# Linear attention with ReLU features on one core: K and V of two groups loaded as one transfer of 256 rows

## Chip, cores and metric

The kernel runs on one core of one Trainium2 chip. The metric is the device time of one execution in microseconds, median of several. The time before is 126.63 us (three runs, 126.61 to 126.84). Engines are TensorE (PE, with its weight loads PEld), VectorE (DVE), ScalarE (ACT), GpSimd (POOL) and SyncE (SP); 16 DMA engines move data between the chip's memory (HBM) and the on-chip memory.

## What is computed

Q, K, V and the output have the shape 8 batches x 12 heads x 512 positions x 64, in fp32: 12.58 MB each. For each of the 96 heads a 64 x 64 matrix and a vector of 64 are summed over all positions of K and V, and each row of Q is multiplied with them.

```python
Q_feat = np.maximum(0, Q)
K_feat = np.maximum(0, K)
KV = np.einsum('bhkd,bhkv->bhdv', K_feat, V)
K_sum = np.sum(K_feat, axis=2)
numerator = np.einsum('bhqd,bhdv->bhqv', Q_feat, KV)
denominator = np.einsum('bhqd,bhd->bhq', Q_feat, K_sum)
return numerator / (denominator[:, :, :, None] + 1e-10)
```

## The kernel before

**Tiling.** Heads are taken in 24 groups of four, and two groups make an octet (12 of them). A group's K is one block of 512 KB in HBM, read as 128 rows of 4 KB: one row is 16 positions of one head, and 32 rows in a column are one head. In the on-chip memory a row is one partition. V is the same. An octet's Q is 1 MB in 128 rows of 8 KB. All loads but those of the first octet's K and V are issued by GpSimd and cast to bf16 on the way, so a K or V tile has 2 KB per partition and a Q tile 4 KB.

**Loads.** The four fp32 loads of groups 0 and 1 (`kv_first`, L106 and L107) are issued by SyncE. GpSimd issues Q of octet 0, then for octets 1 to 11 K, V of the even group, K, V of the odd group, and Q (`load_kv`, L92 to L96; `load_q`, L98; the loop at L110). These instructions stand in GpSimd's queue in this order from the start, each behind the waits for its buffer and for its place among the transfers in flight. The pools `kin` and `vin` have 12 buffers each, `qin` has 7.

**Work of an octet.** Order is written by hand, and each engine runs its instructions in that order.

- `prep(g)` (L133): DVE makes from K the two masked ReLU features (kf, two instructions at L136), and from V the half `vo` at L138. `prep_v` (L141) makes the other half, on ACT for the even group (L143) and on DVE for the odd one (L145).
- `mm_kv(g)` (L148): 16 matmuls sum K features times V into `ps_kv` (L150). `evac_kv` (L156) copies the result of both groups on ACT (L160).
- `qt(o)` (L181): PE transposes Q (L171), ACT applies ReLU (L179).
- `denom(o)` (L218): 16 small matmuls and three DVE instructions (L224, L229, L233) give the reciprocal denominators.
- `out_t(o)` (L193): eight matmuls (L201), copied by ACT (L203).
- `backs(o)` (L283): PE transposes the result back (L239) and DVE multiplies it with the reciprocals, two instructions at L245 (`norm`); then the store.

PSUM tiles of `out_t` and `back` share two buffers (`ps_out`). The loop at L297 runs for o from 0 to 9. For o from 1 to 8 it begins with `kvs(o)`, both `mm_kv` and the evacuation. Then come prep of group 2o+2, `backs(o - 1)`, `denom(o)`, `out_t(o)`, prep of group 2o+3 and `qt(o + 1)`. From o = 8 on `kvs(o + 1)` stands ahead of `qt(o + 1)`, and `backs(o)` behind it. The last two octets are written out from L314 on.

**Stores.** SyncE issues one store of 1 MB per octet (L260), the last octet's in two halves (L258). `store(o)` for o up to 6 is held back: ahead of it SyncE issues a tiny transfer, `scratch`, that reads K of group 2(o + 5) (L253) and so waits until that K tile has landed.

Of the kernel before, what the change touches and what calls it, by code (L numbers as in the profile page):

```python
# [10 lines left out]
def kernel(  # L11
# [7 lines left out]
    nc = tc.nc  # L19
    B, H, S, D = Q.shape  # L20
    assert D == 64
    P = 128
# [4 lines left out]
    R = S * 4 // P  # L27
# [4 lines left out]
    NO = NG // 2  # L32
    assert NO * 8 == NH and R == 16 and RQ == 32
    DELAY = 5
    F32 = 2

    fp32 = mybir.dt.float32
    bf16 = mybir.dt.bfloat16
# [3 lines left out]
    def pool(name, bufs, **kw):  # L42
        return ctx.enter_context(tc.tile_pool(name=name, bufs=bufs, **kw))

    consts = pool("consts", 1)
    qin = pool("qin", 7)
    kin = pool("kin", 12)
    vin = pool("vin", 12)
    kfp = pool("kfp", 4)
    rcp = pool("rcp", 2)  # L50
    outp = pool("outp", DELAY + 2)
# [6 lines left out]
    def view(X, f):  # L58
        return X.rearrange("b h s d -> (b h s d)").rearrange("(n p f) -> n p f", p=P, f=f)

    Qr, Kr, Vr, Or = view(Q, RQ * D), view(K, R * D), view(V, R * D), view(out, RQ * D)
# [27 lines left out]

    q_sb, k_sb, v_sb = {}, {}, {}  # L90

    def load_kv(g):  # L92
        k_sb[g] = kin.tile([P, R, D], bf16, name="k_sb")
        nc.gpsimd.dma_start(out=k_sb[g].rearrange("p r d -> p (r d)"), in_=Kr[g], single_packet=True)  # L94
        v_sb[g] = vin.tile([P, R, D], bf16, name="v_sb")
        nc.gpsimd.dma_start(out=v_sb[g].rearrange("p r d -> p (r d)"), in_=Vr[g], single_packet=True)  # L96

    def load_q(o):  # L98
        q_sb[o] = qin.tile([P, U, 2 * D], bf16, name="q_sb")
        nc.gpsimd.dma_start(out=q_sb[o].rearrange("p u f -> p (u f)"), in_=Qr[o], single_packet=True)  # L100


    for g in range(F32):
        kv = outp.tile([P, 2, R, D], fp32, name="kv_first", tag="o_sb")
# [3 lines left out]
    load_q(0)  # L108
    make_identity(nc, ident)
    for o in range(1, NO):  # L110
        load_kv(2 * o)
        load_kv(2 * o + 1)
        load_q(o)

    def zero(i):
# [198 lines left out]
    o = NO - 2  # L314
    g = 2 * NO - 2
# [52 lines left out]
```

## Time and profile before

| | |
|---|---|
| Median of the runs | 126.63 us (126.61 to 126.84) |
| The profiled execution, its own time | 126.52 us |
| its span, first to last instruction | 124.7 us |
| mean granted TensorE clock | 0.95 |
| PE, PEld busy | 86.0 us, 78.5 us (69%, 63% of the span) |
| DVE, ACT busy | 81.1 us, 79.3 us (65%, 64%) |
| POOL busy (issues of loads mostly) | 33.1 us (27%) |
| HBM read, written | 37.75 MB, 12.58 MB (403 GB/s over the span) |
| K loads by GpSimd | 22, 256 KB each (bf16), 13.9 us from issue to landing |
| V loads by GpSimd | 22, 256 KB each, 13.2 us |
| Q loads | 12, 512 KB each, 14.9 us |
| K issue, V issue on POOL | 578 ns, 597 ns |

A busy share is a mean over the whole span. The page also cuts the span into 40 slices of 3.1 us and gives for each the share of time in which the DMA engines were busy, in tenths (9 is 90% or more), the bytes that they moved per second, and the granted clock of TensorE. Loads that cast count with the bytes that they write, half of what they read. A queue's share is the time that its packets took, over 16 engines' span; packets of one engine overlap a little, so that the shares add up to a little over 100%. In a timeline each line is one or several instructions that follow one another: start, duration, engine, line of the kernel, what it writes and reads, and in brackets how long its engine sat idle before it and what ended that.

The granted clock over the 40 slices is full but for a few: `9999999999999999999769959958999999999996`.

### The profile page before, as it was taken

To read this page: it belongs to the slowest core of one execution; us is meant where nothing else is said; L and a number is where in the kernel's file an instruction comes from. 1 tells how busy PE (TensorE), PEld (TensorE's weight loads), DVE (VectorE), ACT (ScalarE), POOL (GpSimd) and SP (SyncE) were. 2 spreads that over 40 slices of the span, in tenths; PEclk is the share of its full clock that TensorE was granted. 3 is DMA by queue.
4 is the path that set the end of the run, shared out by engine and by line. 5 is a ranking of instruction groups with operands and counts; after the bars stand their busy time and mean duration, and the time that the engine had idled before them with its cause. 6 is when DMAs were issued, how large, how long until landed. Compare 5 with 4: busy or idle time off the path is not lost.

```text
span 124.7 us, 2672 instructions
## 1 busy us (share of the span) xinstructions
PE 86.0 (69%) x1075; PEld 78.5 (63%) x1075; DVE 81.1 (65%) x176; ACT 79.3 (64%) x114; POOL 33.1 (27%) x62
## 2 busy tenths in 40 slices
PE   0041196998989899894598599399777587797600
PEld 0040194997878788793597499299576486696500
DVE  2605743949798897979247845935928918979600
ACT  0251549989898997989249558666839646837100
POOL 6924433415253341142133124034022000000000
PEclk9999999999999999999769959958999999999996
DMA  3999999999999999999999999999999999999993
GB/s 133 322 285 277 216 205 210 213 210 215 207 213 208 210 214 327 257 215 300 282 215 282 302 213 258 324 213 234 342 223 218 322 257 215 319 416 420 426 416 143
DMA packets 10748, 32.68 MB, mean 262 GB/s; under 512 B 1392, under 2 KB 1392, under 8 KB 9328
## 3 DMA queue, kind: packets, MB, share of 16 engines
q0 software_dynamic: 8064, 17.83, 74.7%
q1 hardware_dynamic: 2672, 14.68, 29.2%
q8 instruction: 8, 0.13, 0.4%
q14 instruction: 4, 0.03, 0.1%
HBM read 37.75 MB, written 12.58 MB: 403 GB/s over the span
## 4 chain that ended last, share of the span: by engine, by line
DMA 34%; DVE 26%; PE 25%; ACT 5%; issue 2%; SPq 1%; DVEq 1%; ACTq 0%; POOLq 0%
DMA v_sb<-in_V_dram 14%; DVE o_sb L245 13%; DMA q_sb<-in_Q_dram 13%; PE ps_kv L150 11%; DMA kv_first<-in_V_dram 8%; PE ps_bk L239 6%; PE ps_qt L171 4%; DVE kf L136 3%; ACT qt L179 3%; DVE vo L138 3%; ACT kvd L160 2%; PE ps_ot L201 2%; DVE vo L145 2%; DVE den L229 1%; DVE rec L233 1%
## 5 line engine op out<-in xcount | busy, mean ns | idle before, releaser
L150 PE MATMUL ps_kv<-vo,kf 128*128 128x132 bf16 x384 | 31.3, 247 | 18.4 <-ACT vo L143 7.9
L150 PEld LDWEIGHTS <-kf 128*128 128x128 bf16 x384 | 28.9, 111 | 19.7 <-DVE vo L138 10.3
L245 DVE TENSOR_TENSOR o_sb<-ps_bk,rec 128x1024 f32<-128x1024 f32 x24 | 28.4, 1220 | 16.7 <-PE ps_bk L239 16.7
L160 ACT CAST kvd<-ps_kv 64x260 bf16<-64x260 f32 (+1 forms) x54 | 18.7, 346 | 19.0 <-PE ps_kv L150 16.8
L179 ACT ACTIVATE qt<-ps_qt 128x1024 bf16<-128x1024 bf16 x23 | 22.4, 1027 | 4.9 <-PE ps_qt L171 4.8
L203 ACT COPY ot_sb<-ps_ot 128x1024 f32<-128x1024 f32 x22 | 21.9, 1014 | 2.1 <-PE ps_ot L201 1.3
L239 PE MATMUL ps_bk<-ident,ot_sb 128*128 128x128 f32 x192 | 23.0, 273 | 0.0
L136 DVE TENSOR_SCALAR kf<-k_sb,mask 128x1024 bf16<-128x1024 bf16 x44 | 18.3, 457 | 5.8 <-DMA k_sb<-in_K_dram 5.8
L94 POOL DMA_DIRECT2D k_sb<-in_K_dram x22 | 12.7, 578 | 34.1 <-DMA q_sb<-in_Q_dram 16.8
L239 PEld LDWEIGHTS ps_bk<-ident,ot_sb 128*128 128x128 f32 x192 | 20.8, 141 | 0.0
L171 PE MATMUL ps_qt<-ident,q_sb 128*128 128x128 bf16 x192 | 15.3, 243 | 5.6 <-DMA q_sb<-in_Q_dram 5.6
L96 POOL DMA_DIRECT2D v_sb<-in_V_dram x22 | 13.1, 597 | 19.7 <-DMA k_sb<-in_K_dram 12.0
L171 PEld LDWEIGHTS <-q_sb 128*128 128x128 bf16 x192 | 13.7, 110 | 6.6 <-DMA q_sb<-in_Q_dram 6.4
L201 PE MATMUL ps_ot<-qt,kvd 128*128 128x256 bf16 x88 | 13.5, 284 | 4.0 <-DVE o_sb L245 4.0
L201 PEld LDWEIGHTS <-kvd 128*128 128x128 bf16 x88 | 8.5, 101 | 6.5 <-issue 5.4
L138 DVE TENSOR_SCALAR vo<-v_sb,mask 128x1024 bf16<-128x1024 bf16 x22 | 10.8, 489 | 1.6 <-DMA v_sb<-in_V_dram 1.6
L143 ACT ACTIVATE vo<-v_sb,mask 128x1024 bf16<-128x1024 bf16 x10 | 11.5, 1154 | 0.2
L221 PEld LDWEIGHTS <-qt 128*128 128x128 bf16 x192 | 6.7, 97 | 4.7 <-ACT qt L179 3.4
L221 PE MATMUL ps_den<-kvd,qt 128*128 128x16 bf16 x192 | 7.5, 179 | 2.6 <-ACT qt L179 2.1
L100 POOL DMA_DIRECT2D q_sb<-in_Q_dram x12 | 6.7, 558 | 8.0 <-DMA v_sb<-in_V_dram 5.0
L224 DVE SCALAR_TENSOR_TENSOR own<-ps_den,mask_h 128x256 f32<-128x256 f32 x12 | 5.0, 417 | 3.3 <-PE ps_den L221 3.3
L145 DVE TENSOR_SCALAR vo<-v_sb,mask 128x1024 bf16<-128x1024 bf16 x12 | 5.8, 484 | 0.0
(27 smaller groups left out, 29.5 us busy)
## 6 DMA issues: line engine op xcount, KB each, us to landing
out_dram<-o_sb SPq DMA_DIRECT2D x11, 1024.0 KB, 9.1
q_sb<-in_Q_dram POOLq DMA_DIRECT2D x12, 512.0 KB, 14.9
k_sb<-in_K_dram POOLq DMA_DIRECT2D x22, 256.0 KB, 13.9
v_sb<-in_V_dram POOLq DMA_DIRECT2D x22, 256.0 KB, 13.2
kv_first<-in_K_dram SPq DMA_DIRECT2D x2, 512.0 KB, 5.6
kv_first<-in_V_dram SPq DMA_DIRECT2D x2, 512.0 KB, 7.0
out_dram<-o_sb SPq DMA_DIRECT2D x2, 512.0 KB, 4.9
scratch<-k_sb SPq DMA_DIRECT2D x7, 0.1 KB, 4.8
```

The lines of the kernel that those rows point to most:

```text
L96: nc.gpsimd.dma_start(out=v_sb[g].rearrange("p r d -> p (r d)"), in_=Vr[g], single_packet=True)
L136: nc.vector.tensor_scalar(kf[g][:, :, s, :], k_sb[g], scalar1=0.0, scalar2=mask[:, 0, s:s + 1], op0=Alu.max, op1=Alu.mult)
L138: nc.vector.tensor_scalar(vo[g % NB][:, :, 0, 2:D + 2], v_sb[g], scalar1=mask[:, 1, 0:1], scalar2=None, op0=Alu.mult)
L150: nc.tensor.matmul(ps_kv[:, g % 2, 0:2 * (D + 2)].rearrange("p (t d) -> p t d", t=2), kf[g][:, r, :, :].rearrange("p s d -> p (s d)"), vo[ ...
L160: copy(kvd[o % NK][64 * c:64 * c + 64, 4 * gs.start + s:4 * gs.stop:2, c * D1:c * D1 + D1].rearrange("p (g t) d -> p g t d", t=2), ps_kv[6 ...
L171: nc.tensor.transpose(ps[:, u, :], q_sb[o][:, i * (U // 2) + u, :], ident)
L179: nc.scalar.activation(to, ps, Act.Relu)
L201: nc.tensor.matmul(ps[:, i], kvd[o % NK][:, h, 1:2 * D + 1], q[:, :, h, :], start=True, stop=True, skip_group_check=True)
L203: nc.scalar.copy(ot[o][:, :, 4 * j:4 * j + 4], ps.rearrange("p h u c -> p u h c"))
L221: nc.tensor.matmul(ps[:, u], qt_sb[o % NZ][:, u, :], kvd[o % NK][:, :, 0:2 * D1:2 * D1 - 1], start=True, stop=True, skip_group_check=True)
L239: nc.tensor.transpose(ps[:, 2 * v:2 * v + 2].rearrange("p c d -> p (c d)"), ot[o][:, 8 * j + v].rearrange("p h c -> p (h c)"), ident32)
L245: nc.vector.tensor_tensor(o_sb[:, rs], ps, rec[o][:, rs].unsqueeze(2).to_broadcast([P, 16, D]), op=Alu.mult)
```

## The change

K tiles of the two groups of an octet become one tile of two halves, and V likewise. In octets 1 to 9 each such tile is loaded by one transfer of 256 rows: for each partition p the row p of the first group and the row p of the second, 512 KB apart in HBM, 2 KB each side by side in the tile. In octets 10 and 11 the halves are loaded one by one, in the order of before. The pools have six buffers of the double size instead of twelve. Readers of the tiles take the half that they took before.

```diff
+    PAIRS = NO - 2
...
-    kin = pool("kin", 12)
-    vin = pool("vin", 12)
+    kin = pool("kin", 6)
+    vin = pool("vin", 6)
...
-    def load_kv(g):
-        k_sb[g] = kin.tile([P, R, D], bf16, name="k_sb")
-        nc.gpsimd.dma_start(out=k_sb[g].rearrange("p r d -> p (r d)"), in_=Kr[g], single_packet=True)
-        v_sb[g] = vin.tile([P, R, D], bf16, name="v_sb")
-        nc.gpsimd.dma_start(out=v_sb[g].rearrange("p r d -> p (r d)"), in_=Vr[g], single_packet=True)
+    def load_kv(o):
+        pairs = [(kin.tile([P, 2, R * D], bf16, name="k_sb"), Kr, k_sb),
+                 (vin.tile([P, 2, R * D], bf16, name="v_sb"), Vr, v_sb)]
+        for t, _, sb in pairs:
+            for i in range(2):
+                sb[2 * o + i] = t[:, i].rearrange("p (r d) -> p r d", d=D)
+        if o < PAIRS:
+            for t, X, _ in pairs:
+                nc.gpsimd.dma_start(out=t, in_=X[2 * o:2 * o + 2].rearrange("g p f -> p g f"), single_packet=True)
+        else:
+            for i in range(2):
+                for t, X, _ in pairs:
+                    nc.gpsimd.dma_start(out=t[:, i], in_=X[2 * o + i], single_packet=True)
...
     for o in range(1, NO):
-        load_kv(2 * o)
-        load_kv(2 * o + 1)
+        load_kv(o)
         load_q(o)
```

## The prediction

> **What bounds the kernel now.** I read the slices and the queue table of the page first, then the GpSimd and SyncE timelines, then the waits of DVE and PE in the last third. The page on the DMA engines:
>
> ```profile
> DMA  3999999999999999999999999999999999999993
> GB/s 133 322 285 277 216 205 210 213 210 215 207 213 208 210 214 327 257 215 300 282 215 282 302 213 258 324 213 234 342 223 218 322 257 215 319 416 420 426 416 143
> ...
> q0 software_dynamic: 8064, 17.83, 74.7%
> q1 hardware_dynamic: 2672, 14.68, 29.2%
> ```
>
> The 16 DMA engines are never idle between the second and the last slice. Loads count here by their bf16 bytes, so slices with loads alone (5 to 15, 205 to 216 GB/s) read about 420 GB/s of fp32, the same as the stores of the last slices (416 to 426). The 37.75 MB read and 12.58 MB written at 420 GB/s are 119.8 us of a 124.7 us span. The end is set by how long the DMA engines need for fixed work, as long as no engine runs out of it. The GpSimd timeline between two stores shows the price of one load; its columns are start, duration, engine, line, what, and the wait before it:
>
> ```profile
> 30.60 0.53 POOL L94 DMA_DIRECT2D k_sb<-in_K_dram  x1 [0.72 <-DMA k_sb<-in_K_dram]
> 31.89 0.76 POOL L96 DMA_DIRECT2D v_sb<-in_V_dram  x1 [0.77 <-DMA v_sb<-in_V_dram]
> 34.33 0.53 POOL L94 DMA_DIRECT2D k_sb<-in_K_dram  x1 [1.68 <-DMA q_sb<-in_Q_dram]
> 35.56 0.53 POOL L96 DMA_DIRECT2D v_sb<-in_V_dram  x1 [0.70 <-DMA k_sb<-in_K_dram]
> 36.81 0.53 POOL L100 DMA_DIRECT2D q_sb<-in_Q_dram  x1 [0.72 <-DMA v_sb<-in_V_dram]
> 38.13 0.53 POOL L94 DMA_DIRECT2D k_sb<-in_K_dram  x1 [0.79 <-DMA k_sb<-in_K_dram]
> 39.36 0.53 POOL L96 DMA_DIRECT2D v_sb<-in_V_dram  x1 [0.69 <-DMA v_sb<-in_V_dram]
> 41.78 0.53 POOL L94 DMA_DIRECT2D k_sb<-in_K_dram  x1 [1.89 <-DMA q_sb<-in_Q_dram]
> ```
>
> Each issue waits for the landing of the transfer eight before it, so the spacing of issues is that of landings: 1.23 to 1.3 us behind a K or V (half a MB read), 2.42 to 2.44 where a Q (1 MB) has to land. The wait is always on a landing, not on a buffer: 12 buffers are never all taken. Last, the compute side in the last third (DVE, PE, then SyncE):
>
> ```profile
> 82.78 0.88 DVE L136 TENSOR_SCALAR kf<-k_sb,mask 128x1024 bf16<-128x1024 bf16 x2 [1.60 <-DMA k_sb<-in_K_dram]
> 84.11 0.49 DVE L138 TENSOR_SCALAR vo<-v_sb,mask 128x1024 bf16<-128x1024 bf16 x1 [0.44 <-DMA v_sb<-in_V_dram]
> 86.14 2.36 DVE L245 TENSOR_TENSOR o_sb<-ps_bk,rec 128x1024 f32<-128x1024 f32 x2 [1.54 <-PE ps_bk L239]
> ```
> ```profile
> 60.69 1.68 PE L171 MATMUL ps_qt<-ident,q_sb 128*128 128x128 bf16 x16 [2.53 <-DMA q_sb<-in_Q_dram]
> ...
> 81.70 3.52 PE L150 MATMUL ps_kv<-vo,kf 128*128 128x132 bf16 x32
> ```
> ```profile
> 103.35 11.21 SPq L260 DMA_DIRECT2D out_dram<-o_sb  x5
> 117.71 1.46 SPq L258 DMA_DIRECT2D out_dram<-o_sb  x2
> ```
>
> From 55 to 81 us compute waits for loads. From 81 on it runs without a DMA wait up to the last stores at 117.71, while a queue of finished stores keeps the engines full. The page has no view of single packets; the trace's records of them give the last store's completions between 122.1 and 123.5 us. On three of the 16 engines a gap of 0.25 us lies ahead of it; on the engine that ends last the store before it still ran until 120.9, against 119.6 when the last store could start. So compute has about 1.2 us of room there.
>
> **The change, part by part.**
>
> *Transfers.* 36 K and V transfers become 18, with the same rows of 4 KB read and 2 KB written. The page's 8064 packets of q0 are 56 x 128 rows and 56 x 16 = 896 small ones: one completion write for each transfer and DMA engine. 18 x 16 = 288 of these go. In the packet records such a write takes 20 ns in the mean (22 mostly), and a row follows the one before after 154 ns: 8 x 154 + 21 = 1253 ns for a transfer, which is the spacing above. A pair then takes 16 x 154 + 21 = 2485 ns where two singles take 2506. Each DMA engine saves 18 x 21 ns = **0.38 us**. Bounds: nothing, if the write hides beside rows; above, a Q (2.44 by the timeline) against two singles (1.23 + 1.25 at least), 0.04 to 0.05 a pair, 0.9 us at most. I take 0.38, the records' own number.
>
> By the Trainium skill (DMA: Bandwidth & Descriptors, "Anatomy of one DMA — SWDGE (gpsimd) path") a DMA has about 2 us of fixed cost beside its bytes, which would make 18 fewer transfers worth some 36 us by estimate. The row speaks against it: with eight in flight a K or V costs 1.25 us in all, so nothing of those 2 us is on the path. The same section calls the completion write itself almost free, about a cycle; by that the sum would be nothing rather than 0.38.
>
> *GpSimd.* 18 issues of 0.53 to 1.0 us go, and 18 remain with 256 rows; one costs between 0.53 (as now) and 1.2 (two of 0.59). GpSimd is busy 2.65 of 10 us in an octet, waiting for landings otherwise, so this costs nothing; without that cover it would be at most 18 x 0.6 = 11 us, the other way none. Eight transfers in flight are now up to 2.7 octets instead of 1.6. The pair of octet o+6 needs both groups of octet o consumed, which lies more than two octets back: no new buffer wait.
>
> *Landing order.* Within an octet K, V, K, V, Q becomes KK, VV, Q. Bytes ahead of Q are the same. K of the first group lands 1.25 us later, its V 2.5 us later, K of the second 1.25 us earlier. Three places feel that:
>
> (a) Start. Loads of q0 and the fp32 loads of SyncE take turns by transfer, so the second kv_first V (DVE resumes at 12.08) lands behind 2.49 us of K instead of 1.25: compute starts 1.25 us later. Cover: DVE waits for V at 54, and PE waits 2.53 us for Q at 60.69; both are set by loads, so the shift is gone by then. Without that cover it would be 1.25.
>
> (b) Store gate (L253). Stores 0 to 4 follow a K pair, 1.25 us later; the loads take the place. DMA work is unchanged: 0. Q may land up to 2 us earlier, since the store then arrives after most engines have begun Q.
>
> (c) prep of the first group of each octet. DVE waits in order at L138; behind it stand both norms (L245), the denominator and the second prep, 5.8 us. Until octet 8 Q's wait covers it. In octet 9, the last paired one, V lands two transfers after the 84.11 of now: 86.6, less the 0.38 saved, 86.2 to 86.5; plus 0.4 to 0.5 of L138, norm starts 86.6 to 87.0 instead of 86.14. From there compute has no slack, so the last store is issued **0.5 to 0.85 us** later. That uses up 1.2 - 0.38 = 0.8 us of room: just about covered.
>
> *Sum:* -0.38 on the DMA engines, +0 elsewhere. The profiled execution took 126.52 (124.7 of it the span, 1.8 around it) and would take 126.14; the median of the runs lies 0.11 above, so **126.25 us**, -0.3%.
>
> **Rivals.**
>
> 1. *No change*, 126.6: the completion write was hidden already, or the gain is eaten by (c), or the pair is cut back into two. For: the room and the cost of (c) are equal to 0.1 us. Against: 8 x 154 + 21 fits the spacing only if the write takes its own time.
>
> 2. *Late V and a slower PE in octet 9 become the end.* While DVE waits for V pair 9, PE has finished backs of octet 7 and waits some 2.5 us for a ps_out buffer. After waits of 1.5 to 2.5 us the granted clock fell now (slices at 0.5 to 0.7; 32 matmuls of L150 took 3.52 us at 81.70 against 1.9 to 2.1 at full clock). If the fall reaches the second group of octet 9 it adds 0.7 for 16 matmuls and 0.3 to 0.6 for the transposes (1.23 to 1.68 against 0.9 to 1.06). With 0.85 that is 1.9 us on the last store's issue: 1.9 - 1.2 = 0.7 past the present end, some **127.2**. It decides from 1.2 us of delay on. For: PE idled and lost its clock in three octets before. Against: at 100.4, after a wait of 1.54, it did not; much of a fall would lie on out_t, which waits anyway.
>
> 3. *Rows 512 KB apart read worse.* A pair alternates between two blocks of 512 KB. From 1.3 ns (0.9%) per row on, the gain is gone. The slices with loads alone lie at 205 to 216 around 211; if pairs went at the worst of them, 3% of 18 x 2.49 us is 1.3: **127.5**. For: nothing in this trace has this pattern. Against: a Q of 1 MB costs no less per byte. The Trainium skill (the same page, "Latency and other measured facts") reports 207 against 214 GB/s for a row pitch of 512 KiB, also 3%, but with 128 rows in step; no run here shows it.
>
> 4. *The full 0.9 us*, 125.8, if two transfers cost as much more than a Q as the timeline lets one read.
>
> **How the numbers follow.** Forecast 0.5; no change 0.22; rival 2 0.13; rival 3 0.10; rival 4 0.05. About 0.2% (0.25 us) is what a measurement of this kernel can tell from none. The forecast's own range is 125.9 to 126.5, a tenth of its chance above 126.38: faster 0.45 + 0.05 = 0.50, same 0.05 + 0.21 = 0.26, slower the rest, 0.24. Range 125.8 to 127.2: from rival 4 to rival 2, leaving rival 3 out.
>
> **What would show it.** q0 with 7776 packets, 288 fewer, and its share down by about 0.3 points; K and V issues 2.49 apart; eight in flight as before; DVE's wait at L138 in octets 6 to 9 with norm at 86.6 to 87.0; the last stores issued near 118.3, landing about as long after. Wrong if the DMA row shows a gap, if spacing of pairs is above 2.51, or if the last stores land in under 4 us, which would mean compute sets the end.

## The result, and the profile after

| | before | after |
|---|---|---|
| Median of 21 runs each | 126.61 us | 127.19 us |
| Lowest to highest | 126.31 to 127.19 | 126.94 to 128.14 |
| The profiled execution, its span | 126.52, 124.7 us | 127.11, 125.3 us |
| Mean granted PE clock | 0.95 | 0.93 |

The changed kernel takes 1.0048 of the time before (95% interval 1.0033 to 1.0063): 0.6 us slower, where 0.38 us faster was forecast. An execution over 1.5% above the fastest of its kernel counts as slow and is left out below: one of e5 (168.36 us, the one profiled, so that e5's profile is not used) and one of e6 (129.88 us).

Slices and queues of the changed kernel, as shown of before:

```profile
DMA  3999999999999999999999999999999999999992
GB/s 141 323 279 271 212 213 211 216 207 220 207 213 210 211 219 259 292 220 264 316 213 246 337 214 213 318 267 213 329 254 216 343 239 216 339 421 424 429 392 102
...
q0 software_dynamic: 7776, 17.83, 74.5%
q1 hardware_dynamic: 2672, 14.68, 29.2%
```

q0 has the 288 packets less that were forecast. Slice 15 (47 to 50 us), with the first store in it, moved 259 GB/s where the kernel before moved 327. Issues on GpSimd (start, duration, line, what, the wait ahead):

```profile
29.14 0.56 POOL L109 DMA_DIRECT2D q_sb<-in_Q_dram  x1 [1.19 <-DMA k_sb<-in_K_dram]
31.57 0.70 POOL L101 DMA_DIRECT2D k_sb<-in_K_dram  x1 [1.88 <-DMA v_sb<-in_V_dram]
34.04 0.71 POOL L101 DMA_DIRECT2D v_sb<-in_V_dram  x1 [1.77 <-DMA q_sb<-in_Q_dram]
36.60 0.56 POOL L109 DMA_DIRECT2D q_sb<-in_Q_dram  x1 [1.84 <-DMA k_sb<-in_K_dram]
```

A pair's issue costs 0.7 us instead of two of 0.59. The spacing of issues in these rows is 2.43 to 2.56 for every kind of transfer now. In the records of single packets, which no view shows, completions of pairs follow each other after 2485 to 2486 ns, where two singles took 2506.

DVE, PE and SyncE around octet 9 and at the end:

```profile
84.20 0.88 DVE L144 TENSOR_SCALAR kf<-k_sb,mask 128x1024 bf16<-128x1024 bf16 x2 [2.09 <-DMA k_sb<-in_K_dram]
86.73 0.49 DVE L146 TENSOR_SCALAR vo<-v_sb,mask 128x1024 bf16<-128x1024 bf16 x1 [1.65 <-DMA v_sb<-in_V_dram]
87.13 2.35 DVE L253 TENSOR_TENSOR o_sb<-ps_bk,rec 128x1024 f32<-128x1024 f32 x2
```
```profile
88.40 0.60 PE L209 MATMUL ps_ot<-qt,kvd 128*128 128x256 bf16 x4 [1.63 <-DVE o_sb L253]
89.53 0.88 PE L209 MATMUL ps_ot<-qt,kvd 128*128 128x256 bf16 x4 [0.54 <-DVE o_sb L253]
90.20 3.51 PE L158 MATMUL ps_kv<-vo,kf 128*128 128x132 bf16 x32
```
```profile
103.83 12.13 SPq L268 DMA_DIRECT2D out_dram<-o_sb  x5
119.11 1.46 SPq L266 DMA_DIRECT2D out_dram<-o_sb  x2
```

V of octet 9 is now waited for 1.65 us, norm starts at 87.13 instead of 86.14, PE waits 1.63 us for it and runs the 32 matmuls behind in 3.51 us. The last stores are issued 1.40 us later. That is the picture of rival 2, and yet it is not where this execution lost its time: the packet records have the last completion at 123.66 us, against 123.51 before. Only 0.15 to 0.2 us of the 0.6 lie ahead of it. They are work of the DMA engines: the time that these lose against a steady 428 GB/s is 0.19 us less than before from 12.5 to 45 us, 0.42 us more from 45 to 52.5 us, where the first store is, and 0.09 us less from there to 110 us. The rest is behind the last store, in the closing instructions. Of these the view of their line gives number, durations, and first and last start; before the change:

```profile
L363 SPq DRAIN  x3: 7/7/7, 123.9 to 124.2; - x3
...
L363 POOLq EVENT_SEMAPHORE_RANGE_CLEAR  x1: 140/140/140, 124.3 to 124.3; - x1
```

and after:

```profile
L371 SPq DRAIN  x3: 7/7/7, 124.1 to 124.8; - x3
...
L371 POOLq EVENT_SEMAPHORE_RANGE_CLEAR  x1: 139/139/139, 124.9 to 124.9; - x1
```

SyncE's first DRAIN follows the last store's landing; GpSimd's clearing of the semaphores came 0.4 us after it before, 0.8 us now. The records show the gap between the first two of GpSimd's closing instructions: 0.08 us before, 0.41 now. Only the end of the kernel follows there.

So three losses stand against the saving: (A) the late V of octet 9, (B) the dip at the first store, (C) GpSimd's closing gap.

### The profile page after: what moved, and what is told of

The parts are those of the page before. It is cut to its first block, busy times and chain, and to the rows that moved or that the text cites. A ratio compares the mean times of both kernels' runs of the same rounds, so it can differ in the third digit from the quotient of the medians.

```text
span 125.3 us, 2644 instructions
## 1 busy us (share of the span) xinstructions
PE 87.1 (69%) x1075; PEld 79.7 (64%) x1075; DVE 81.2 (65%) x176; ACT 78.9 (63%) x114; POOL 24.9 (20%) x44
## 3 DMA queue, kind: packets, MB, share of 16 engines
q0 software_dynamic: 7776, 17.83, 74.5%
## 4 chain that ended last, share of the span: by engine, by line
DVE 32%; DMA 30%; PE 26%; ACT 4%; issue 2%; SPq 1%; DVEq 1%; ACTq 0%
DMA v_sb<-in_V_dram 22%; DVE o_sb L253 17%; PE ps_kv L158 12%; DMA kv_first<-in_V_dram 8%; PE ps_bk L247 8%; DVE kf L144 4%; PE ps_qt L179 3%; DVE vo L146 3%; ACT kvd L168 2%; DVE vo L153 2%; DVE den L237 2%; DVE own L232 2%; ACT qt L187 2%; PE ps_ot L209 1%; DVE rec L241 1%
## 5 line engine op out<-in xcount | busy, mean ns | idle before, releaser
L158 PE MATMUL ps_kv<-vo,kf 128*128 128x132 bf16 x384 | 30.7, 244 | 17.3 <-ACT vo L151 7.9
L158 PEld LDWEIGHTS <-kf 128*128 128x128 bf16 x384 | 28.3, 110 | 18.7 <-DVE vo L146 10.7
L209 PE MATMUL ps_ot<-qt,kvd 128*128 128x256 bf16 x88 | 14.3, 295 | 10.6 <-DVE o_sb L253 10.6
L179 PE MATMUL ps_qt<-ident,q_sb 128*128 128x128 bf16 x192 | 16.6, 254 | 0.0
L179 PEld LDWEIGHTS <-q_sb 128*128 128x128 bf16 x192 | 15.3, 117 | 0.5
L101 POOL DMA_DIRECT2D v_sb<-in_V_dram x9 | 6.6, 731 | 15.3 <-DMA q_sb<-in_Q_dram 9.1
L101 POOL DMA_DIRECT2D k_sb<-in_K_dram x9 | 6.5, 720 | 11.8 <-DMA v_sb<-in_V_dram 7.8
```

Of the source, the lines that this page charges most:

```text
L101: nc.gpsimd.dma_start(out=t, in_=X[2 * o:2 * o + 2].rearrange("g p f -> p g f"), single_packet=True)
L158: nc.tensor.matmul(ps_kv[:, g % 2, 0:2 * (D + 2)].rearrange("p (t d) -> p t d", t=2), kf[g][:, r, :, :].rearrange("p s d -> p (s d)"), vo[ ...
L179: nc.tensor.transpose(ps[:, u, :], q_sb[o][:, i * (U // 2) + u, :], ident)
L209: nc.tensor.matmul(ps[:, i], kvd[o % NK][:, h, 1:2 * D + 1], q[:, :, h, :], start=True, stop=True, skip_group_check=True)
```

## The experiments

All times are medians, taken beside runs of the kernel before on the same chip, which gave 126.50 to 126.63 in these groups. The ratios, with their 95% interval, are against those runs and go with the means: a few long executions raise a ratio and leave the median where it is.

**Which octets are paired.** e1 and e2 change one number, e3 pairs nothing but keeps the double tiles:

```diff
-    PAIRS = NO - 2
+    PAIRS = NO - 3    # e1
+    PAIRS = 5         # e2
+    PAIRS = 0         # e3
```

> Octet 9 loads its four transfers one by one again; octets 1 to 8 stay paired. Theory A (the late V of octet 9 and the lower PE clock behind it move the last stores, which set the end): the last stores are issued near 117.7 us as before the change instead of 119.1, and the time falls to 126.3 to 126.5. Theory B (the DMA engines lose 0.45 us once, near 47 us, when the first store meets the deeper queue of loads): that stall is still there, last stores land as in the changed kernel, 127.0 to 127.2. Theory C (0.33 us are lost behind the last store, in GpSimd's closing instructions): unchanged, 127.0 to 127.2.

> Only octets 1 to 4 are paired. Theory A: 126.4 to 126.5 (8 completion writes of 21 ns less than before the change, no late V in the last third). Theory B: the queue in front of the first store holds single transfers, so there is no stall near 47 us: 126.4 to 126.5 as well. Theory C: the closing gap depends on how many instructions GpSimd has; it may stay, 126.8.

> The double tiles and six buffers stay, but every half is loaded by its own transfer, in the order of before. All three theories: 126.6 as before the change, within 0.15. If it is near 127.2 the tiles and buffers cost the time and not the transfers.

Measured: e1 126.79 (1.0009, 0.9995 to 1.0023), e2 126.46 (0.9981, 0.9966 to 0.9996), e3 126.55 (0.9979, 0.9956 to 1.0002). The tiles and buffers cost nothing. Against e3, which should equal the kernel before, e2 gains 0.1 at most. e1 has no late V in octet 9 and is still 0.3 to 0.5 above what theory A alone asks for; its last stores are issued at 118.47, where 117.7 was expected.

**GpSimd's closing instructions.** Small memsets behind the last load, 28 (e4), 2 (e5) and 128 (e11):

```diff
+    fill = consts.tile([P, 1], bf16, name="fill")
+    for i in range(28):
+        nc.gpsimd.memset(fill, 0.0)
```

> The changed kernel with 28 small memsets on GpSimd behind its last load, so that GpSimd has as many instructions as before the change. Theory C: the gap in GpSimd's closing instructions is gone and the time is 0.33 lower, 126.85. Theories A and B: 127.2, no change.

> The changed kernel with 2 small memsets on GpSimd instead of 28. If the 0.33 us in GpSimd's closing instructions depends on where its last instructions fall, and not on the work, two instructions are enough: the gap is gone, 126.8 to 126.85 as with 28. If it takes as many instructions as before the change, the gap stays, 127.2.

> The changed kernel with 128 memsets on GpSimd. If the closing gap comes from where the last instructions of GpSimd fall on a grid of up to 128 instructions, it is there again, 0.33 to 0.36 us. If it is a matter of too few instructions, it is gone, 0.

> The changed kernel once more, for a second profile. Theory B: rows of the K pair of octet 6 again take up to 0.6 us near 47 us, 0.4 to 0.5 us lost on the DMA engines. Theory C: the gap of 0.33 in GpSimd's closing instructions is there again. Theory A: the last stores are issued later than 118 us.

Measured: e4 126.81 (1.0021, 1.0000 to 1.0041) and e5 126.82 (1.0011, 0.9991 to 1.0031): 0.37 to 0.38 us less than the changed kernel, for two instructions more or 28. e11, one execution: 127.14. e8, the changed kernel again, one execution: 127.26. The closing lines of e4, then of e11:

```profile
L374 SPq DRAIN  x3: 7/7/7, 124.9 to 125.2; - x3
...
L374 POOLq EVENT_SEMAPHORE_RANGE_CLEAR  x1: 142/142/142, 125.3 to 125.3; - x1
```
```profile
L374 SPq DRAIN  x3: 7/7/7, 124.2 to 124.8; - x3
...
L374 POOLq EVENT_SEMAPHORE_RANGE_CLEAR  x1: 139/139/139, 124.9 to 124.9; - x1
```

0.4 us in e4, 0.7 in e11. The trace lists 74 GpSimd instructions in the changed kernel and 202 in e11, and both have the gap (0.41 and 0.44 in the two profiles of the changed kernel, 0.39 in e11); 76, 84, 92 and 102 instructions (e1, e2, e3, and e4 or the kernel before) leave 0.08. Theory C holds, and too few instructions are not the cause, since 202 have the gap too. 74 and 202 are 128 apart, so a place on a grid of 128 or a divisor of it fits; two counts with the gap don't prove that rule. What is fetched or waited for there the trace doesn't show.

**The dip at the first store.** e6 adds to e4 a later gate for store 0, e7 leaves octet 6 unpaired, e15 adds an early scratch transfer:

```diff
-            nc.sync.dma_start(out=scratch, in_=k_sb[2 * (o + DELAY)][0:1, 0, :])
+            nc.sync.dma_start(out=scratch, in_=k_sb[2 * (max(o, 1) + DELAY)][0:1, 0, :])   # e6
...
-        if o < PAIRS:
+        if o < PAIRS and o != 6:                                                            # e7
...
+        if o == 0:                                                                          # e15
+            nc.sync.dma_start(out=scratch, in_=k_sb[8][0:1, 0, :])
```

> The changed kernel with 28 memsets, and store 0 held until K of octet 6 has landed, together with store 1, instead of octet 5. Theory B1 (the slow rows near 47 us come with the first store): they move to about 55 to 57 us, same size, time unchanged at 126.8. Theory B2 (they belong to the K pair of octet 6, or to that moment): they stay at 47 us. Theory A alone: nothing at 47, time as in the kernel with 28 memsets.

> The changed kernel with 28 memsets, octet 6 loaded by four transfers of 128 rows, the other eight octets paired. Theory B1: slow rows stay near 47 us and hit the first rows there, 126.8. Theory B2 (K pair of octet 6): they are gone, 126.4. Theory A: unchanged.

> The changed kernel with 28 memsets and one more scratch transfer on SyncE, released by K of octet 4, some 7 us ahead of store 0. If the slow rows near 47 us come with the first transfer that SyncE issues after its long pause, they move to about 38 to 40 us or are gone. If they come with the first store itself, they stay near 47 us, 2.5 to 6 us in sum over the engines.

Windows of the changed kernel, then of e6 (stretch, length, busy us of each engine, clock, DMA share, GB/s); up to 48.2 us only loads run in both, but for the tiny rows of `scratch` in the first. The single line behind them is the kernel before, whose first store began at 47.1:

```profile
45.00:47.00 2.00, 1.77 (x31) 1.65 (x29) 2.00 (x7) 2.00 (x3) 0.23 (x1) 1.00 1.07 216
47.00:48.20 1.20, 1.20 (x17) 1.20 (x15) 0.39 (x1) 0.47 (x3) 0.54 (x1) 1.00 1.12 150
```
```profile
45.00:47.00 2.00, 1.79 (x24) 1.78 (x24) 1.44 (x4) 1.32 (x3) 0.14 (x1) 1.00 1.03 210
47.00:48.20 1.20, 1.07 (x10) 0.90 (x9) 0.96 (x1) 1.13 (x4) 0.56 (x1) 1.00 1.10 207
```
```profile
47.00:48.20 1.20, 1.20 (x15) 1.20 (x13) 0.32 (x2) 0.63 (x2) 0.53 (x1) 1.00 1.05 335
```

In the changed kernel the DMA share is as high as ahead of it, but the rate falls to 150 GB/s: rows take longer. In the records 33 rows take up to 533 ns there, instead of 173 for K and V and 324 for Q, 6.5 us too long in sum, 0.4 us for each of the 16 engines; the store's own rows begin at 48.2. With the store one octet later the dip is gone and none of its size appears later (0.4 us in sum near 55 us; at most 1.3 in the other kernels with that gate). In e7 it stays (4.6 us in sum), so it doesn't belong to the pair of octet 6; in e15 it stays at 47.1 to 48.3 us (3.4 us in sum) though SyncE's first transfer ran at 40.8. Hence it comes with the first store at about 47 us, or with the `scratch` transfer right ahead of it, which e15 leaves in its place (47.6 to 48.2 us); but such a store alone is not enough, as the kernel before has one at 47.1. Times: e6 126.62 (1.0025, 0.9995 to 1.0055), e7 126.77 (1.0023, 1.0006 to 1.0039), e15 127.14 (1.0062, 1.0031 to 1.0092). e15 is 0.33 above e4 for another reason: in the records its end comes 1.81 us behind the last landing, against 1.24 before the change and 1.37 in e4, since seven of SyncE's closing waits, 0.06 us each, come only after it. The nine profiles of kernels with octets 5, 7 and 8 paired and store 0 at its old gate all have the dip, 2.5 to 8.7 us in sum; e2 has 1.8, the kernel before and e3 have 0.1.

**What is left without the three losses.** e9 is e1 with the later store 0, e10 the kernel before with it:

> Pairs in octets 1 to 8, octet 9 by single transfers, and store 0 held until K of octet 6 has landed. If the three losses found (slow rows with the first store, late V in octet 9, the closing gap of GpSimd) are all of them, none is left here, and 16 completion writes of 21 ns are saved: 126.25 to 126.35, 0.25% faster than before the change. If the late V is no loss of its own: the same as with pairs to octet 9 and the later store, 126.4 to 126.7, with single runs above 127.4.

> The kernel before the change, with store 0 held until K of octet 6 has landed. It tells whether the later store is a gain by itself. If it only takes away the slow rows of the paired kernels: 126.6 as before. If it helps any kernel: 126.4 or less.

Measured: e9 126.51 (0.9992, 0.9981 to 1.0004), e10 126.61 (1.0005, 0.9986 to 1.0024). The later store is no gain by itself. e9 is level with the kernel before, where the 16 saved writes of 21 ns should give 0.33: between 0.24 faster and 0.05 slower. In the records, measured against a steady 428 GB/s, e9's DMA engines lose 0.44 us between 12.5 and 45 us (e10, with the same gate: 0.62), which is the saving of nine pairs in full, 0.11 up to 52.5 us (0.15), and 1.21 from there to 110 us (1.23), where the last pairs save almost nothing. So 0.24 of the 0.33 reached the DMA engines. Why the rest did not, and why the median shows still less, is open.

**The late V of octet 9 and PE's clock.** Most kernels without closing gap and with octet 9 paired have a tail: above 127.4 us lie 3 of 12 runs of e4, 3 of 11 of e6 and 2 of 12 of e7, but none of 11 of e5. Of e1, e2, e3 and e9, with octet 9 single, it is none of 48; of e10 it is 1 of 12. The profile of e4 fell on one at 127.53:

```profile
88.10 2.14 PE L212 MATMUL ps_ot<-qt,kvd 128*128 128x256 bf16 x8 [2.82 <-DVE o_sb L256]
90.03 1.66 PE L161 MATMUL ps_kv<-vo,kf 128*128 128x132 bf16 x16
...
101.07 1.63 PE L161 MATMUL ps_kv<-vo,kf 128*128 128x132 bf16 x16 [1.54 <-DVE vo L156]
102.50 1.91 PE L182 MATMUL ps_qt<-ident,q_sb 128*128 128x128 bf16 x16
```
```profile
120.00 1.46 SPq L269 DMA_DIRECT2D out_dram<-o_sb  x2
```

PE runs its matmuls at half clock both behind the wait for the late norm (1.66 for 16) and again in octet 10 (1.63, and 1.91 for transposes that take 1.06), and the last stores are issued at 120.00. A fall in octet 10 alone does not make a long run: the records of the granted clock have one at 98.7 to 99.5 us in e3, e10 and e1 as well, whose profiled executions took 126.38, 126.62 and 126.97. The next kernels were to keep PE busy in these waits. e12 put idle matmuls of the kernel's own helper into octet 8's iteration; e13 (on e4) and e14 (on e6) write unread columns of ps_kv; e16 (on e6) and its control e17 (on the kernel before) fill the next wait too:

```diff
         denom(o)
+        if o == SAME:
+            for i in range(20):
+                nc.tensor.matmul(ps_kv[:, 0, 132:256], ident, ident[:, 0:124], start=True, stop=True,
+                                 skip_group_check=True)
         out_t(o)
...
     def kvs(o):
         mm_kv(2 * o)
+        if o > SAME:
+            fill_pe(18)
         mm_kv(2 * o + 1)
```

> The changed kernel with 28 memsets on GpSimd, and 12 matmuls without use on PE between the denominators and the output matmuls of octet 8, where PE waits for the late norm; what they write is never read. Theory A with the clock: PE keeps its clock, the 32 matmuls of octet 9 take 2.1 to 2.4 us instead of 3.5, the last stores are issued at 118.1 to 118.4, and the runs above 127.4 (3 of 12 with 28 memsets alone) are gone; the median 126.75. If the clock is not the cause of those runs, they stay.

> The changed kernel with 28 memsets on GpSimd and 20 matmuls without use on PE ahead of the output matmuls of octet 8; they write columns of ps_kv that nothing reads and wait for nothing. Theory A with the clock: the clock stays at full there, the 32 matmuls of octet 9 take 2.1 to 2.6 us, the last stores are issued at 118.0 to 118.4, no run above 127.4, median 126.7. If the clock is not the cause, 2 to 4 of 12 runs above 127.4 remain.

> The same with store 0 held until K of octet 6 has landed, so with none of the three losses and all nine pairs: 126.3 to 126.45, no run above 127.4; if it is no better than with pairs to octet 8 and the later store (126.51), the rest of the saving is lost elsewhere.

> As e14 (changed kernel, 28 memsets, store 0 later, PE filled in octet 9), with 18 matmuls without use on PE also between the two groups of octets 9 and 10, where PE waits for the second V. If the remaining slow runs are clock falls in octet 10 (the profile of the run with 28 memsets at 127.53 shows one), they are gone or nearly: at most 1 of 12 above 127.4, median 126.35 to 126.5. If 3 of 12 remain, the clock is not their cause.

> The kernel before the change with the same matmuls without use on PE. If before the change compute has room enough at the end, they change nothing: 126.55 to 126.65. If they help any kernel: 126.4 or less.

e12 took 129.30 (1.0210, 1.0175 to 1.0246) and told nothing of the clock, since its matmuls share a tile with the denominators and so waited for DVE:

```profile
89.50 2.72 PE L199 MATMUL ps_den<-q_sb,ident 128*128 128x256 bf16 x12 [3.46 <-DVE own L235]
```

e13: 126.78 (1.0027, 1.0007 to 1.0047), 3 of 12 above 127.4; e14: 126.60 (1.0023, 0.9994 to 1.0052), 3 of 12. In the profile of e13 the clock held (1.11 us for 16 matmuls of octet 9) and the last stores were issued at 118.35, which is what the late V alone was priced at; the tail stayed, but none of its long executions was profiled. In the profile of e14 (126.54) the clock fell at 88.12 in spite of the fill. e16 took 127.42 (1.0071, 1.0050 to 1.0091) and its control 127.69 (1.0090, 1.0071 to 1.0109): the fills cost about as much on the kernel before, so they settle nothing. In e16 the clock fell in spite of them:

```profile
85.37 1.24 PE L302 MATMUL ps_kv<-ident 128*128 128x124 bf16 x20
...
89.43 1.70 PE L161 MATMUL ps_kv<-vo,kf 128*128 128x132 bf16 x16
90.92 2.06 PE L302 MATMUL ps_kv<-ident 128*128 128x124 bf16 x18
```

Nor is it only the clock that e17 changed: it has the dip at the first store too (7.6 us in sum, 45.5 to 49.0 us), with no pair in it. What the dip needs besides a first store at that time is therefore not the pairs themselves, and stays open. So does the tail's cause: shown is that it comes mostly with octet 9 paired, and that one such run had PE's clock fall twice. That the late V can set the end once the other two losses are gone is shown by e6's profile (126.97): from 12.5 to 118 us its DMA engines lost as little as those of e9 (1.83 and 1.84 us), but its last stores were issued at 119.43, e9's at 116.91, and the last one landed at 123.82, e9's at 123.33.

## Why the prediction was wrong, point by point

The step that failed is the sum's "+0 elsewhere": it put at nothing two things that the change moved, GpSimd's closing instructions and the rows around the first store. The table gives medians as differences from the kernel before that ran beside them, in us. Two kernels that should not differ from it, e3 and e10, lie at -0.08 and +0.07, so that steps below 0.1 are not told from none.

| What is taken away | from | to |
|---|---|---|
| the closing gap of GpSimd | changed kernel, +0.58 | e4 +0.18, e5 +0.23 |
| the dip at the first store | e4 +0.18; e1 +0.16; e13 +0.20 | e6 +0.03; e9 -0.03; e14 +0.02 |
| the late V of octet 9 | e4 +0.18; e6 +0.03 | e1 +0.16; e9 -0.03 |

From the forecast, -0.38, to the changed kernel, +0.58, it is 0.96. The closing gap has 0.35 to 0.40 of it and the dip 0.15 to 0.19; most of the rest is the saving itself, which the time of e9 does not show either.

- **Transfers, -0.38.** The step was right as far as it could be read directly: 7776 packets, and 2485 ns for a pair. In e9 the whole of it reached the DMA engines up to 45 us (0.18 of 0.19 us), and 0.24 of 0.33 up to 110 us. In the time no more than that is seen even there, and perhaps nothing: this term is not confirmed, and what became of it is open. By the Trainium skill (DMA: Bandwidth & Descriptors, "Anatomy of one DMA — SWDGE (gpsimd) path") the completion write is nearly free; 21 ns less for each engine and pair says that it is not quite.
- **GpSimd, "this costs nothing".** This step cost the most. The issues cost nothing, as said (0.7 us each, waits as before), but the shorter program moved GpSimd's closing instructions, and these are on the path once the last store has landed: 0.33 us in the profile, 0.35 to 0.40 in the table. It is about two thirds of the 0.6 us.
- **(b) Store gate, "DMA work is unchanged: 0".** This failed second. The bytes are unchanged, but rows went slow around the first store: 0.41 us per engine in the profile, 0.15 to 0.19 in the three comparisons of the table. In each of them the intervals of the two ratios overlap; that all three agree speaks for the loss. The other half was right: in the records Q of octet 8 landed at 78.9 instead of 80.3 us, and PE's wait for Q is gone.
- **(a) Start.** Compute was to start 1.25 us later; DVE resumed at 12.18 instead of 12.08. The fp32 V landed by 12.15 and so ahead of the first pair's K (12.60 on): turns by transfer, as the step had them, are not what happened. No effect on the sum.
- **(c) Late V.** Forecast 86.6 to 87.0 for norm, measured 87.13, since the saving that was to bring V forward had gone into (b). The delay of the last stores was mis-sized, 1.40 for 0.5 to 0.85, as the clock fell; with the clock held, in e13, it was 0.64. The room was mis-sized too: where the late issue set the end, in the profiles of e4 and e6, the last landing came 4.38 to 4.39 us after it, and before the change 5.80, so that the room was 1.4 and not 1.2. In the changed kernel 4.55 are left, and the DMA engines still set the landing. The room is used up in the tail, as in e4's profile (issue 120.00, 127.53). In the medians this step is not told from nothing. (The rows behind L138 take 5.0 us, from 86.14 to 91.15, and not 5.8; no term rests on it.)
- **Rivals.** Rival 2 had the right place and mechanism and happened in the profile, but was not what set the median; that its 127.2 is the 127.19 measured is chance. Rival 3 is out: a pair's rows 512 KB apart followed each other as fast as before, after 154 ns. Rival 4 is out too: a pair took 21 ns less on the engines than two singles, and not 50. Rival 1 names e9's result, but not the changed kernel's. The two losses that decided were in no rival.
- **"Wrong if ..."** The DMA row shows no gap, pairs followed each other after 2.49 us in the records, and the last store landed 4.55 us after its issue: none of the three signs came, since they looked neither at the length of single rows nor behind the last store. Of the signs for the forecast, the issue of the last stores near 118.3 failed (119.11).

## What to carry to other kernels

A kernel that keeps its DMA engines full gains at most what a merge takes off the engines themselves, here 21 ns a transfer, and not the latency of the transfers it saves. A saving that small has to be weighed against everything that a shorter program moves: the order of landings, the moment at which the first store meets the loads, and the closing instructions behind the last store. Before a cause is named from one profile, shift it alone: two memsets and one later gate told more here than the two profiles side by side.

## What the runs showed of the hardware

- The first step of GpSimd's closing took 0.31 to 0.36 us more with 74 and with 202 instructions than with 76, 84, 92 or 102.
- Near the first store, load rows of 4 KB took up to 0.74 us (e1) instead of 173 ns, for 1.2 to 1.9 us, in some programs and not in others, while the DMA share still read full (1.12 at 150 GB/s in the changed kernel): the share counts a slow packet as busy.
- PE's granted clock fell to half for 3.41 us or a multiple of it, after waits as short as 1.54 us (e4, octet 10), and in e16 although 20 matmuls filled half of the wait. The Trainium skill (TensorE: Matmul & The Clock Gate, "Why this matters for your kernels") advises against gaps above about 3 us; here shorter ones were enough, in some executions.
- Matmuls put in to keep PE busy cost the kernel before 1.2 us (e17); its last store landed between 122.6 and 124.9 us over the engines, against 122.1 to 123.5 without them.
